# Hybrid HGRN2/mLSTM layer with a seven-product SwiGLU network: product order in a block, finer steps at the network's seams, scan steps moved

## Chip, cores and metric

One core of one Trainium2 chip runs one denoising step of one layer. The metric is the device time of an execution in microseconds, the median of several runs. The shapes are fixed: 128 context tokens and 1024 latent tokens (1152 in all, nine tiles of 128), model width 1024, network width 2816 (22 blocks of 128), everything in fp32.

## The reference, cut to what matters

Each token is normalised and modulated, projected into two groups of heads (four HGRN2 heads, four mLSTM heads, both scanned forward and backward in chunks), the heads' outputs are normed and gated and projected back, and a SwiGLU network follows. Context and latent tokens take different modulation rows; the latent scans start from cached states.

```python
def trunk_layer(x, cond, ...):
    mod = (jax.nn.silu(cond) @ w_mod_l + b_mod_l)[:, None, :]
    sh1, sc1, g1, sh2, sc2, g2 = jnp.split(mod, 6, axis=-1)
    h = rmsnorm(x, n1) * (1.0 + sc1) + sh1
    mix, new_states = token_mix(h, ...)      # projection, two scans, head norms, w_out
    x = x + g1 * mix
    h = rmsnorm(x, n2) * (1.0 + sc2) + sh2
    ffn = (jax.nn.silu(h @ w_gate_l) * (h @ w_up_l)) @ w_down_l
    x = x + g2 * ffn
    return x, new_states
...
y_prompt = rmsnorm(xp, final_norm_w)
y_sample = rmsnorm(xs, final_norm_w)
```

## The kernel before

Every large matmul is made of three fp32r matmuls: each operand is cast by ScalarE to a high part, VectorE subtracts that from the original for a low part, and TensorE adds up high*high, high*low and low*high in one PSUM bank (`three`, `product`). PSUM is cut into three banks for the pool `psA` and five for `psB`.

The program has five stages. In the first (`ORDER0`) the tokens are normed, transposed and modulated and the first projection runs. In the second (`ORDER`) the other projections, the convolution, both scans and the late modulation rows (`late_mod`) are steps with names such as `m.0.E.0`: head kind, head, step, third of the tokens. Both orders are strings of step names written out by hand; the steps are emitted in that order, and a scheduler then places the instructions of each engine in its own queue by dependencies and priorities that follow the order of emission. `m.h.E.r` only issues two loads on SyncE's queue (`eb` and `qt`, rows of `rows_d` spread over partitions), which `m.h.O1.r` needs on VectorE; `out.i.q` loads half of a tile of mixed heads and splits it. The third stage is the output projection (`out_main`, `po` in PSUM) with the residual, the second norm, the transposes (`nt` in PSUM) and the modulation of each tile in `out_post`.

The fourth and fifth stages are the network, in two passes of 22 blocks: p=0 with 640 tokens, p=1 with 512. A block works on its 2x2 split in a scheme with seven products instead of eight (`block`, matmuls at L1285, `gu` in PSUM). The left operands are the tokens (a11, a12, a22 and the sums s1 to s4, built by `left_build`), the right ones the weights (b11, b21, b22 and the sums t1 to t4, built by `right_build`). The left tiles have names beginning with `a_` and `s_`, and the right ones are `Tb` for a pair whose first member is a plain block of weights and `Tt` for a pair that begins with a sum. Pairs of right operands share a buffer of two tags (`wh`, `wl`), and the sums t1 to t4 are written to DRAM (`t_d`) in pass 0 and loaded from there in pass 1 by GpSimd's queue. `r` are the raw weights in a ring of four buffers, `wraw`.

A block's code calls, after each product, one of the seven pieces of the next block's `right_build` (`nx`), one down-projection `unit` of the group before (six matmuls, `dn` in PSUM, added to `acc` by VectorE) and the `extra` pieces of that place, `more(0)` to `more(6)`. The last product's evacuation (`finish`) and two pieces of `right_build` are run at the head of the next block. The tiles 7 and 8 are finished inside block 0 of pass 0: `out_post(7)` at `more(2)`, `out_post(8)` at `more(6)`. All seven pieces of `left_build(1)`, for pass 1, stand among the ten last down units of pass 0. At the end, `last` takes each of eight final down units from PSUM: a multiply by the gate row `g2` into `y`, an add to `acc`, a square on ScalarE, and for each tile the reciprocal root on GpSimd, two multiplies by it and `fnrow` (L128), and the store. `residual` multiplies what has been added up by `g2` and adds the residual row `x1`; half of these steps stand between the last down units.

## Time and profile before

| what | value |
|---|---|
| median of 3 runs | 1663.03 us (1661.39 to 1663.47) |
| the profiled execution | 1657.22 us, of which the span of the trace is 1655.4 us |
| TensorE busy | 1586.9 us (96% of the span) |
| VectorE busy | 1196.2 us (72%) |
| ScalarE busy | 696.3 us (42%) |
| stages, us from the start | first 0 to 55, scans to 750, output projection to 852, pass 0 to 1281, pass 1 and tail to 1655.4 |

The profile is of one execution. A sum of parts is made against its own time, 1657.22 us, and carried to the median by the difference. The page shows the whole span in slices; the timeline gives the instructions of a stretch in order of time, with what ended the idle time before each; the windows view gives busy time and TensorE's granted clock of any stretch. Matmuls are pipelined, so a row of twelve matmuls with 1.92 us is followed by the next 1.76 us after its start.

### The profile page before, as it was taken

The page shows a single profiled execution, that of the slowest core. Times are in us where ns is not written, and L with a number is a line of the kernel's source. Part 1 is how long each engine was busy: PE and PEld are TensorE (multiplying, and loading weights), DVE is VectorE, ACT ScalarE, POOL GpSimd, SP SyncE. Part 2 cuts the span into 40 slices and gives each one's busy share as a digit, 9 for nine tenths or more (in the row PEclk, how much of TensorE's full clock was granted, in tenths as well). Part 3 has the DMA queues.
Part 4 walks back from the last instruction along what each step waited for, and adds up shares of the span by engine and source line. Part 5 has one row for each costly group of instructions (what it writes and reads, how often), then busy time and mean ns, then how long its engine had stood idle before and what let it go on. Part 6 is the DMA issues. An engine that isn't in the chain of part 4 may idle for free.

```text
span 1655.4 us, 31292 instructions
## 1 busy us (share of the span) xinstructions
PE 1586.9 (96%) x11993; PEld 1434.6 (87%) x11993; DVE 1196.2 (72%) x2620; ACT 696.3 (42%) x1657; POOL 152.0 (9%) x264
## 2 busy tenths in 40 slices
PE   7999999999999989989989999999999999999996
PEld 5998898988898989857768999999998999999995
DVE  6765676577985776765666888888887866766677
ACT  6623433354454545453655433333434343333332
POOL 1000000000010000001111111111111111111110
PEclk9999999999999999999999999999999999999998
DMA  8312213112243234365457665556567677877762
GB/s 325 115 31 73 78 56 92 54 56 88 89 137 101 65 76 93 83 196 175 134 190 244 212 204 187 192 184 202 180 202 242 217 230 244 257 229 240 240 209 96
DMA packets 123466, 261.51 MB, mean 158 GB/s; under 512 B 12444, under 2 KB 39476, under 8 KB 122292
## 3 DMA queue, kind: packets, MB, share of 16 engines
q1 hardware_dynamic: 90916, 155.69, 30.2%
q0 software_dynamic: 28176, 101.73, 18.6%
q10 hardware_dynamic: 4224, 2.10, 0.4%
q8 instruction: 94, 1.54, 0.4%
q14 instruction: 56, 0.46, 0.1%
HBM read 194.69 MB, written 64.77 MB: 157 GB/s over the span
## 4 chain that ended last, share of the span: by engine, by line
PE 80%; DVE 7%; DMA 6%; issue 3%; ACT 2%; POOL 1%; SPq 0%; another core or an unknown queue 0%; DVEq 0%; POOLq 0%; ACTq 0%
PE gu L1285 28%; PE dn L135 16%; PE pv L135 5%; PE po L984 5%; PE zm L135 5%; PE zg L135 3%; PE zb L135 2%; DMA qt<-rows_d 2%; PE zo L135 2%; DMA wm<-in_dram 2%; PE zq L135 2%; PE zf L135 2%; PE z L333 2%; PE lm L196 1%; PE mo L891 1%
## 5 line engine op out<-in xcount | busy, mean ns | idle before, releaser
L135 PE MATMUL dn<-hid 128*128 128x512 f32 x1188 | 306.9, 395 | 4.4 <-ACT hid L1292 4.2
L135 PEld LDWEIGHTS dn<-hid 128*128 128x128 f32 x1188 | 214.2, 189 | 41.3 <-ACT hid L1292 5.4
L1285 PE MATMUL gu<-s,Tb 128*128 128x320 f32 (+1 forms) x1584 | 235.1, 297 | 0.8 <-ACT Tb L1096 0.6
L1285 PEld LDWEIGHTS gu<-s,Tb 128*128 128x128 f32 x1584 | 222.5, 190 | 6.4 <-ACT Tb L1096 0.9
L125 DVE TENSOR_TENSOR tmp<-gu,tmp 128x320 f32<-128x320 f32 (+1 forms) x308 | 136.2, 454 | 72.0 <-PE gu L1285 69.5
L1096 ACT CAST Tb<-r 128x512 fp32r<-128x512 f32 x176 | 106.9, 620 | 144.7 <-PE gu L1285 79.4
L1285 PE MATMUL gu<-a,Tb 128*128 128x320 f32 (+1 forms) x1056 | 156.4, 297 | 0.0
L1285 PEld LDWEIGHTS gu<-a,Tb 128*128 128x128 f32 x1056 | 148.8, 190 | 3.8
L125 DVE TENSOR_TENSOR acc<-acc,dn 128x512 f32<-128x512 f32 x172 | 117.8, 685 | 22.2 <-PE dn L135 22.1
L119 DVE TENSOR_TENSOR Tb<-r,Tb 128x512 fp32r<-128x512 f32 x176 | 119.6, 688 | 17.8 <-ACT Tb L1096 15.0
L984 PE MATMUL po<-wo_A,mix 128*128 128x512 f32 x288 | 95.6, 405 | 2.0 <-ACT mix L213 1.5
L1255 ACT CAST hid<-raw_dn 128x512 fp32r<-128x512 f32 x88 | 52.7, 618 | 73.0 <-PE dn L135 62.4
L135 PE MATMUL pv<-wh_v,h_hi 128*128 128x256 f32 (+1 forms) x288 | 82.8, 288 | 0.0
L135 PE MATMUL pv<-wl_v,h_hi 128*128 128x256 f32 (+1 forms) x288 | 82.2, 286 | 0.0
L135 PE MATMUL pv<-wh_v,h_lo 128*128 128x256 f32 (+1 forms) x288 | 81.8, 284 | 0.0
L128 DVE SCALAR_TENSOR_TENSOR qk<-pad,sm,qk 128x384 f32<-128x384 f32 (+1 forms) x144 | 78.3, 570 | 0.9
L1285 PEld LDWEIGHTS gu<-a,Tt 128*128 128x128 f32 x528 | 74.8, 189 | 3.3
L1285 PEld LDWEIGHTS gu<-s,Tt 128*128 128x128 f32 x528 | 74.8, 189 | 3.3
L1285 PE MATMUL gu<-a,Tt 128*128 128x320 f32 (+1 forms) x528 | 77.3, 296 | 0.0
L1285 PE MATMUL gu<-s,Tt 128*128 128x320 f32 (+1 forms) x528 | 77.3, 296 | 0.0
L168 POOL TENSOR_TENSOR rs_f<-ms_f,half 128x3 f32<-128x3 f32 x24 | 22.8, 949 | 532.7 <-DVE ms_f L166 495.1
L119 DVE TENSOR_TENSOR hid<-raw_dn,hid 128x512 fp32r<-128x512 f32 x88 | 60.3, 688 | 11.7 <-ACT hid L1255 11.7
(338 smaller groups left out, 3456.3 us busy)
## 6 DMA issues: line engine op xcount, KB each, us to landing
r<-in_dram SPq DMA_DIRECT2D x154, 256.0 KB, 4.1
t_d<-Tb POOLq DMA_DIRECT2D x44, 512.0 KB, 3.8
raw_dn<-in_dram SPq DMA_DIRECT2D x88, 256.0 KB, 3.1
t_d<-Tt POOLq DMA_DIRECT2D x44, 512.0 KB, 4.6
Tb<-t_d POOLq DMA_DIRECT2D x44, 512.0 KB, 4.7
Tt<-t_d POOLq DMA_DIRECT2D x44, 512.0 KB, 5.9
wm<-in_dram SPq DMA_DIRECT2D x64, 256.0 KB, 3.8
wm<-in_dram SPq DMA_DIRECT2D x8, 1024.0 KB, 7.9
```

Of the source, the lines that this page charges most:

```text
L119: V.tensor_tensor(out=out, in0=a, in1=b, op=ALU.subtract)
L125: V.tensor_tensor(out=out, in0=a, in1=b, op=ALU.add)
L128: V.scalar_tensor_tensor(out=out, in0=a, scalar=s, in1=b, op0=op0, op1=op1)
L135: E.matmul(ps, a, b, start=(i == 0), stop=(i == n - 1))
L168: G.tensor_tensor(out=rs, in0=ms, in1=half[:, 0:n], op=ALU.pow)
L196: E.matmul(ps[32 * j:32 * j + 32, :], cT[:, 4 * g + j, :], rhs, start=(g == 0), stop=(g == 1), tile_position=(0, 32 * j))
L333: E.matmul(first[b][r], x, y, start=(k == 0 and n == 0), stop=(k == KD - 1 and n == 2))
L891: E.matmul(po[:, d, :], eb[:, d, cs], v[:, c, :], start=True, stop=(ch == 0))
L984: E.matmul(ps[n], mt[:, a, k, :], b[:, k, nn], start=(k == 0 and m == 0), stop=(k == KD - 1 and m == 2))
L1096: S.copy(hi, src)
L1255: S.copy(hi, draw[u, n])
L1285: E.matmul(ps, rt[:, x, k, :], lt[:, y, k, :], start=(n == 0), stop=(n == 11))
```

## The change

1. The seven products of a block stand in another order. Before: a11 b11, s2 t2, a12 b21, s3 t3, s1 t1, a22 t4, s4 b22. After: a11 b11, a12 b21, s2 t2, s3 t3, s1 t1, a22 t4, s4 b22. The pairs of right operands become (b11, b21), (t2, t3), (t1, t4), (b22); the split of b21 moves from the third piece of `right_build` to the second, t2 from the second to the third. `left_build` is cut into ten pieces, with a11 and a12 first.
2. `out_post` is cut in two; the transposes and the modulation become `out_turn`. In block 0 `out_post(7)` stands at place 1, `out_turn(7)` at 4, `out_post(8)` at 5, and `out_turn(8)` at place 1 of block 1.
3. Seven pieces of `left_build(1)` stay among the last down units of pass 0, now behind the unit's add; three move to places 0 to 2 of block 0 of pass 1.
4. At the end, the last two blocks of `w_dn` are multiplied by the `g2` row before their split (four VectorE multiplies), and `last` is one add from PSUM. The other half of the residual steps moves into the last block (two of four in its places, two behind it). The last units run tile by tile, 8, 8, 7, 7, 6, 6, 5, 5.
5. Both tables of steps are permuted by a few places; `m.0.E.0`, for instance, stood behind `m.0.KV.0` and now stands behind `m.1.zm.1.2`.

The number of matmuls is the same, and so is that of transfers of `t_d`; VectorE has four instructions fewer at the end.

```diff
-lateb.10 late.11.B m.1.cv.1.0 m.0.KV.0 m.0.E.0 vproj.2.4 m.0.E.1 m.1.cv.1.1 m.0.O1.0 m.0.O1.1 vproj.2.8
+vload.2 g.3.zg.1 m.1.zm.1.0 g.3.O.1 g.3.zg.2 lateb.9 m.1.zm.1.1 m.1.zm.1.2 m.0.E.0 late.10.B g.3.F.0 m.0.states
...
-    slots = {"a11": "a12", "s2": "s3", "a12": "s1", "s3": "a22", "a22": "s4", "s4": "s2", "s1": "a11"}
+    slots = {"a11": "s2", "a12": "s3", "s2": "s1", "s3": "a22", "a22": "s4", "s4": "a12", "s1": "a11"}
...
-        def first():
+        def sums():
             for a, ks in ext_parts(p):
                 add(a, source(p, 1, 0)[:, ks, :], source(p, 1, 1)[:, ks, :])
-            left_split(p, "a11", one(0, 0))
-
-        def second():
+
+        def differences():
             sub(source(p, 1, 0), source(p, 0, 0), source(p, 1, 0))
             for a, ks in ext_parts(p):
                 sub(source(p, 0, 0)[:, ks, :], a, source(p, 0, 0)[:, ks, :])
-            left_split(p, "s2", one(0, 0))
-
-        def third():
-            left_split(p, "a12", one(0, 1))
-            sub(source(p, 0, 1), source(p, 0, 1), source(p, 0, 0))
-
-        return [first, second, third, lambda: left_split(p, "s3", one(1, 0)), lambda: left_split(p, "a22", one(1, 1)),
+
+        return [lambda: left_split(p, "a11", one(0, 0)), lambda: left_split(p, "a12", one(0, 1)), sums, differences,
+                lambda: left_split(p, "s2", one(0, 0)),
+                lambda: sub(source(p, 0, 1), source(p, 0, 1), source(p, 0, 0)),
+                lambda: left_split(p, "s3", one(1, 0)), lambda: left_split(p, "a22", one(1, 1)),
                 lambda: left_split(p, "s4", one(0, 1)), lambda: left_split(p, "s1", ext_parts(p))]
...
         def first():
-            right_pair(u, "wh", ("b11", "t2"))
+            right_pair(u, "wh", ("b11", "b21"))
...
         def second():
+            right_split(u, "b21", r("r21"))
             if not again:
                 sub(r("r11"), r("r22"), r("t1"))
+                sub(r("r12"), r("r22"), r("r12"))
+
+        def third():
+            right_pair(u, "wl", ("t2", "t3"))
             summed("t2", wraw.get((u, "r11")))
-
-        def third():
-            right_pair(u, "wl", ("b21", "t3"))
-            right_split(u, "b21", r("r21"))
-            if not again:
-                sub(r("r12"), r("r22"), r("r12"))
-
-        def fourth():
             if not again:
                 sub(r("r21"), r("r21"), r("r11"))
+
+        def fourth():
             summed("t3", wraw.get((u, "r12")))
...
     def down_split(u, f, n):
         hi, lo = down_of(f, n)
+        if u >= 2 * NF - 2:
+            mul(draw[u, n], draw[u, n], g2[1][:, n * 512:n * 512 + 512])
         S.copy(hi, draw[u, n])
...
     def last(i, n, ps):
         nn = slice(n * 512, (n + 1) * 512)
-        y = fp.tile([P, 512], F32, tag="rw", name="y%d_%d" % (i, n), bufs=4)
-        mul(y, ps, g2[1][:, nn])
-        add(acc_of(i, nn), acc_of(i, nn), y)
+        add(acc_of(i, nn), acc_of(i, nn), ps)
...
             if p == 0 and f == 0:
-                extra.setdefault(2, []).append(lambda: out_post(NT - 2))
-                extra.setdefault(6, []).append(lambda: out_post(NT - 1))
+                extra.setdefault(1, []).append(lambda: out_post(NT - 2))
+                extra.setdefault(4, []).append(lambda: out_turn(NT - 2))
+                extra.setdefault(5, []).append(lambda: out_post(NT - 1))
+            if p == 0 and f == 1:
+                extra.setdefault(1, []).append(lambda: out_turn(NT - 1))
...
-            if p == 1 and f == NF - 1:
+            if p == 1 and g == NG - 1:
                 for j, i in enumerate(tiles_of(p)):
-                    extra.setdefault(1 + j, []).append(lambda i=i: x1_load(i, 0))
-                    extra.setdefault(3 + j, []).append(lambda i=i: residual(i, 0))
+                    extra.setdefault(j, []).append(lambda i=i: x1_load(i, odd))
+                    if not odd or j < 2:
+                        extra.setdefault(j + 3, []).append(lambda i=i: residual(i, odd))
...
-            pend = None
-            for i, n in ((8, 0), (7, 0), (8, 1), (7, 1), (6, 0), (5, 0), (6, 1), (5, 1)):
-                if n:
-                    x1_load(i, 1)
-                ps = down_unit(p, g, i, n, True)
-                if n:
-                    residual(i, 1)
-                last(i, n, ps)
+            for i in tiles_of(p)[2:]:
+                residual(i, 1)
+            for i in tiles_of(p):
+                for n in range(2):
+                    last(i, n, down_unit(p, g, i, n, True))
```

TensorE's queue at the start of the network, before: `gu_0` are the products of block 0, told apart by their left operand, and the two `nt` are the halves of tile 7's transposes.

```order
L1285 MATMUL gu_0_9649<-a_0_9341,Tb_0_9452 128x320 x12
L1285 MATMUL gu_0_9663<-s_0_9347,Tb_0_9452 128x320 x12
L1285 MATMUL gu_0_9677<-a_0_9442,Tb_0_9561 128x320 x12
L1178 MATMUL nt_0_9708<-con,xj_9695 128x128
L1178 MATMUL nt_1_9718<-con,xj_9695 128x128
L1285 MATMUL gu_0_9730<-s_0_9446,Tb_0_9561 128x320 x2
L1178 MATMUL nt_0_9708<-con,xj_9695 128x128
```

The same place after:

```order
L1291 MATMUL gu_0_9649<-a_0_9337,Tb_0_9452 128x320 x12
L1291 MATMUL gu_0_9663<-a_0_9340,Tb_0_9452 128x320 x12
L1291 MATMUL gu_0_9691<-s_0_9442,Tt_0_9561 128x320 x12
L1291 MATMUL gu_0_9710<-s_0_9446,Tt_0_9561 128x320 x12
L1291 MATMUL gu_0_9728<-s_0_9556,Tt_0_9628 128x320 x12
L1180 MATMUL nt_0_9746<-con,xj_9676 128x128
L1180 MATMUL nt_1_9756<-con,xj_9676 128x128
L1291 MATMUL gu_0_9768<-a_0_9449,Tt_0_9628 128x320 x5
```

Two products stood whole behind the first one ahead of the transposes of tile 7, and now four do.

TensorE's queue at the head of block 1, after; `dn_0` are down units of group 0, which need `hid` of block 0, and the `nt` here are tile 8's transposes (before, these stood at once behind block 0's last product):

```order
L1291 MATMUL gu_0_9803<-s_0_9553,Tb_0_9635 128x320 x11
L1291 MATMUL gu_1_9819<-a_0_9337,Tb_1_9704 128x320 x12
L1291 MATMUL gu_1_9851<-a_0_9340,Tb_1_9704 128x320 x12
L135 MATMUL dn_0_4_0_10034<-hid 128x512 x2
L135 MATMUL dn_0_3_0_10067<-hid 128x512 x2
L135 MATMUL dn_0_2_0_10093<-hid 128x512
L1180 MATMUL nt_0_9868<-con,xj_9788 128x128
L1180 MATMUL nt_1_9878<-con,xj_9788 128x128
```

Two whole products and five matmuls of down units now stand between block 0's last product and tile 8's transposes.

VectorE's queue in block 12 of pass 0, before: `Tb_13_12028` is the low part of b21 of block 13 (from `r_13_11930`, the raw r21).

```order
L125 TENSOR_TENSOR tmp_0_9647<-gu_12_11933,tmp_0_9647 128x320
L119 TENSOR_TENSOR Tb_13_11972<-r_13_11869,Tb_13_11972 128x512
L125 TENSOR_TENSOR acc<-acc,dn_5_4_0_11946 128x512
L119 TENSOR_TENSOR r_13_11869<-r_13_11928,t_13_11975 128x512
L119 TENSOR_TENSOR hid<-raw_dn_1_11956,hid 128x512
L125 TENSOR_TENSOR tmp_0_9648<-gu_12_11959,tmp_0_9647 128x320
L119 TENSOR_TENSOR Tb_13_11972<-r_13_11869,Tb_13_11972 128x512
L125 TENSOR_TENSOR acc<-acc,dn_5_3_0_11977 128x512
L125 TENSOR_TENSOR tmp_0_9647<-gu_12_11987,tmp_0_9647 128x320
L119 TENSOR_TENSOR Tb_13_12028<-r_13_11930,Tb_13_12028 128x512
```

After, where b21 is the second half of `Tb_13_11973`:

```order
L125 TENSOR_TENSOR tmp_0_9648<-gu_12_11933,tmp_0_9647 128x320
L119 TENSOR_TENSOR Tb_13_11973<-r_13_11869,Tb_13_11973 128x512
L125 TENSOR_TENSOR acc<-acc,dn_5_4_0_11946 128x512
L119 TENSOR_TENSOR Tb_13_11973<-r_13_11930,Tb_13_11973 128x512
L119 TENSOR_TENSOR r_13_11869<-r_13_11928,t_13_11976 128x512
L125 TENSOR_TENSOR tmp_0_9647<-gu_12_11960,tmp_0_9647 128x320
```

The subtraction that needs r21 stood behind the evacuations of the second and third products of block 12 (`gu_12_11959`, `gu_12_11987`), and now it stands ahead of that of the third one emitted (`gu_12_11960`), with one down unit's add between the evacuation before it and itself.

VectorE's queue at the end, before, from the first of the last down units:

```order
L122 TENSOR_TENSOR y_0_17638<-dn_10_8_0_17631,g2row 128x512
L122 TENSOR_TENSOR y_0_17651<-dn_10_7_0_17644,g2row 128x512
L125 TENSOR_TENSOR acc<-acc,y_0_17638 128x512
L125 TENSOR_TENSOR acc<-acc,y_0_17651 128x512
L122 TENSOR_TENSOR y_1_17668<-dn_10_8_1_17659,g2row 128x512
L125 TENSOR_TENSOR acc<-acc,x_8_1_17657 128x512
L122 TENSOR_TENSOR y_1_17693<-dn_10_7_1_17684,g2row 128x512
L125 TENSOR_TENSOR acc<-acc,y_1_17668 128x512
L122 TENSOR_TENSOR y_0_17713<-dn_10_6_0_17706,g2row 128x512
L125 TENSOR_TENSOR acc<-acc,x_7_1_17682 128x512
L125 TENSOR_TENSOR fsq_17641<-fsq_17641 128x1
L125 TENSOR_TENSOR acc<-acc,y_0_17713 128x512
```

After:

```order
L125 TENSOR_TENSOR acc<-acc,dn_10_8_0_17651 128x512
L119 TENSOR_TENSOR hid<-tmp_1_13913,hid 128x256
L125 TENSOR_TENSOR acc<-acc,dn_10_8_1_17662 128x512
L125 TENSOR_TENSOR acc<-acc,dn_10_7_0_17681 128x512
L125 TENSOR_TENSOR fsq_17659<-fsq_17659 128x1
L166 TENSOR_SCALAR ms_fin_17673<-fsq_17659 128x1
L128 SCALAR_TENSOR_TENSOR acc<-acc,rs_fin_17675,fnrow 128x512 x2
L125 TENSOR_TENSOR acc<-acc,dn_10_7_1_17692 128x512
L125 TENSOR_TENSOR acc<-acc,dn_10_6_0_17710 128x512
L125 TENSOR_TENSOR fsq_17689<-fsq_17689 128x1
L166 TENSOR_SCALAR ms_fin_17703<-fsq_17689 128x1
L125 TENSOR_TENSOR acc<-acc,dn_10_6_1_17721 128x512
```

The multiplies into `y` and the adds of `x` are gone from this stretch.

## Rows read from the trace of the kernel before

**Rows 1.** The page's first two parts: busy time of each engine with its share of the span and its instructions, and TensorE's granted clock in 40 slices of the span, in tenths of full speed.

```profile
PE 1586.9 (96%) x11993; PEld 1434.6 (87%) x11993; DVE 1196.2 (72%) x2620; ACT 696.3 (42%) x1657; POOL 152.0 (9%) x264
...
PEclk9999999999999999999999999999999999999998
```

**Rows 2.** The windows view by stage: length of the stretch, then busy us (and instructions) of TensorE, its weight loads, VectorE, ScalarE and GpSimd, the granted clock, the DMA share and GB/s.

```profile
55.00:750.00 695.00, 665.98 (x6311) 605.76 (x6310) 488.51 (x1283) 301.79 (x872) 35.49 (x46) 0.99 0.31 87
750.00:852.00 102.00, 100.57 (x452) 76.66 (x451) 58.82 (x83) 51.92 (x111) 11.54 (x20) 1.00 0.51 165
852.00:900.00 48.00, 37.79 (x233) 34.49 (x232) 31.51 (x59) 25.64 (x53) 6.54 (x12) 0.93 0.63 213
900.00:1277.00 377.00, 377.00 (x2236) 351.50 (x2235) 307.42 (x559) 147.20 (x281) 42.68 (x80) 1.00 0.61 202
1277.00:1284.00 7.00, 4.29 (x18) 3.19 (x17) 7.00 (x12) 4.42 (x8) 0.00 (x0) 0.90 0.60 210
1284.00:1639.00 355.00, 355.00 (x2424) 329.89 (x2422) 255.37 (x506) 124.81 (x257) 48.59 (x90) 1.00 0.69 221
1639.00:1655.40 16.40, 0.07 (x1) 0.00 (x0) 10.51 (x21) 2.52 (x8) 2.02 (x3) 0.56 0.42 160
```

**Rows 3.** The same view of short stretches in which, or just behind which, TensorE waited.

```profile
690.00:695.00 5.00, 5.00 (x19) 3.07 (x16) 0.96 (x1) 1.41 (x5) 0.00 (x0) 0.50 0.33 118
860.00:865.00 5.00, 0.00 (x0) 0.00 (x0) 3.69 (x6) 3.76 (x6) 1.63 (x3) 0.78 0.34 138
865.00:870.00 5.00, 3.90 (x16) 2.94 (x17) 1.86 (x4) 3.33 (x9) 1.14 (x2) 0.54 0.48 185
1280.00:1283.00 3.00, 1.83 (x7) 1.53 (x8) 3.00 (x7) 2.39 (x4) 0.00 (x0) 0.94 0.23 81
1283.00:1286.00 3.00, 3.00 (x10) 2.44 (x9) 3.00 (x6) 0.46 (x1) 0.00 (x0) 0.50 0.57 191
```

**Rows 4.** The timeline of the start of the feed-forward network: start in us, duration in us, engine, line, operation, output and inputs, shape, count, and in brackets the engine's idle time before it and what ended that.

```profile
852.93 1.92 PE L1285 MATMUL gu<-a,Tb 128*128 128x320 f32 x12
...
855.22 0.86 SPq L1163 DMA_DIRECT2D xj<-in_dram  x2
...
859.95 1.23 DVE L125 TENSOR_TENSOR xj<-xj 128x1024 f32<-128x1024 f32 x1 [0.58 <-DMA xj<-in_dram]
...
861.21 1.06 ACT L1170 ACTIVATE xj<-xj 128x1024 f32<-128x1024 f32 x1 [3.95 <-DVE xj L125]
...
862.10 1.22 DVE L125 TENSOR_TENSOR xj<-xj 128x1024 f32<-128x1024 f32 x1
...
864.16 0.57 POOL L168 TENSOR_TENSOR rs_n<-ms_n,half 128x1 f32<-128x1 f32 x1
...
865.30 0.75 DVE L1172 TENSOR_SCALAR xj<-xj,rs_n 128x1024 f32<-128x1024 f32 x1
...
866.10 0.69 PE L1178 MATMUL nt<-con,xj 128*128 128x128 f32 x2 [7.74 <-DVE ms_n L166]
```

**Rows 5.** The timeline at the end of the network's first block and in its second.

```profile
887.68 1.92 PE L1285 MATMUL gu<-s,Tb 128*128 128x320 f32 x12
...
889.44 1.92 PE L1285 MATMUL gu<-a,Tb 128*128 128x320 f32 x12
...
896.63 0.73 PE L135 MATMUL dn<-hid 128*128 128x512 f32 x2 [1.50 <-ACT hid L1292]
```

**Rows 6.** The timeline of the seam between the network's two passes.

```profile
1272.00 1.22 DVE L125 TENSOR_TENSOR ext<-src 128x1024 f32<-128x1024 f32 x1 [2.56 <-DMA src<-hB_d]
...
1280.14 0.49 DVE L122 TENSOR_TENSOR tmp<-tmp,tmp 128x320 f32<-128x320 f32 x1
...
1281.17 3.83 PE L135 MATMUL dn<-hid 128*128 128x512 f32 x11 [2.71 <-ACT hid L1292]
```

**Rows 7.** The timeline of the end of the program.

```profile
1627.84 11.23 PE L135 MATMUL dn<-hid 128*128 128x512 f32 x48
...
1630.25 1.38 DVE L122 TENSOR_TENSOR y<-dn,g2row 128x512 f32<-128x512 f32 x2 [0.26 <-PE dn L135]
...
1645.33 0.69 DVE L125 TENSOR_TENSOR acc<-acc,x 128x512 f32<-128x512 f32 x1
...
1646.84 0.63 ACT L1403 ACTIVATE fjk<-acc 128x512 bf16<-128x512 f32 x1 [0.60 <-DVE fsq L125]
...
1649.55 0.55 POOL L168 TENSOR_TENSOR rs_fin<-ms_fin,half 128x1 f32<-128x1 f32 x1 [1.85 <-DVE ms_fin L166]
1650.13 1.41 DVE L128 SCALAR_TENSOR_TENSOR acc<-acc,rs_fin,fnrow 128x512 f32<-128x512 f32 x2 [0.73 <-POOL rs_fin L168]
```

**Rows 8.** The timeline at three places of the scan phase.

```profile
533.92 0.96 DVE L122 TENSOR_TENSOR qt<-qt,qk 128x768 f32<-128x768 f32 x1 [0.73 <-DMA qt<-rows_d]
...
617.58 0.80 PE L891 MATMUL mo<-v,eb 128*128 128x130 f32 x2 [3.93 <-DVE eb L128]
...
689.59 1.07 PE L196 MATMUL lm<-wm,cT 128*32 128x256 f32 x4 [3.54 <-DMA wm<-in_dram]
```

**Rows 9.** The timeline of an undisturbed block of pass 0 (the SPq row is four DMA issues, the last of them at its end), and behind it the page's sixth part for the same loads: issues, KB each, median us from issue to landing.

```profile
1077.97 9.63 SPq L1087 DMA_DIRECT2D r<-in_dram  x4
...
1090.28 0.69 DVE L125 TENSOR_TENSOR acc<-acc,dn 128x512 f32<-128x512 f32 x1
...
r<-in_dram SPq DMA_DIRECT2D x154, 256.0 KB, 4.1
```

103 lines of the change are left out of this document (57 added, 46 removed).

## The prediction, made before the changed kernel ran

> **What bounds the kernel now.** I read the page's shares first. TensorE is busy 1586.9 us of the 1655.4 us span, so all its waits together are 68.5 us; VectorE has 72% and ScalarE 42% [rows 1]. The share says nothing of where the waits are, so the windows view by stage comes next. In the network's two passes TensorE is busy 377.00 of 377 us and 355.00 of 355 us [rows 2]: no instruction that is taken from another engine there can save time, and the new product order has as many matmuls as the old. What can be saved lies in four places: 10.2 us idle in the 48 us at the start of the network (37.79 busy), 2.7 us between the passes (4.29 of 7), 16.3 us behind the last matmul, and 29.0 us scattered over the 695 us of projections and scans [rows 2]. Then I read what a wait costs beyond itself. Behind each longer one the granted clock shows half speed, 1.2 instead of 2.4 GHz, for some us: 0.54 in 865 to 870, 0.50 in 1283 to 1286, 0.50 in 690 to 695 [rows 3]. With 3.90 us busy at 0.54 the first of these lost some 3.90 x 0.46 = 1.8 us of work at full speed, the second 1.5 us, the third 2.5 us.
>
> **Start of the network.** Before, the first product starts at 852.93, products follow each other 1.76 us apart (887.68, 889.44), and three of them stand ahead of the transposes of tile 7; TensorE has done these at 858.4 and stands until 866.10, 7.74 us [rows 4, 5]. The chain that ends there is the load of the residual (issued 855.22), the add at 859.95, the square at 861.21, GpSimd's root at 864.16, the multiply at 865.30 [rows 4]. After, five products stand ahead, since a12 b21 and s3 t3, s1 t1 do not need tile 7: the fifth is done at 852.93 + 5 x 1.76 + 0.16 = 861.9. The chain still begins with the same load, so it is not much earlier. It loses one piece: tile 8's add (862.10, 1.22 us), which stood on VectorE between tile 7's square and its mean, is now emitted later. From the square's end (862.3) I count 0.5 us for the read of the sum and the mean, 0.57 us root, 0.75 us multiply and some 0.4 us of handing over, which gives transposes at 864.5, a wait of 2.6 us; if the chain gains nothing, 866.1 and 4.2 us. I take 3: minus 4.7 us. The clock I leave as it is, since a wait of 2.71 us at 1281.17 was followed by half speed as well [rows 3, 6]; 0 to minus 1.8. The Trainium skill, in TensorE: Matmul & The Clock Gate, section HAM oscillation, warns only of idle gaps in front of TensorE that are long enough, and by that rule the shortened wait could leave the clock up and the sum would be 1.8 us lower; the row at 1281 speaks against it.
>
> Behind it a second wait of 1.50 us stood at 896.63, where the first down units wanted `hid` of block 0, 7.2 us after that block's last product had ended at 889.4 [rows 5]. Now five matmuls of such units stand only two products (3.5 us) behind it, ahead of tile 8's transposes, and whatever they wait for holds up these too. Against that, tile 8's residual and norm are now worked off before block 0's last product ends, instead of on VectorE and ScalarE just where `hid` is made. Bounds: 0 us, or 7.2 - 3.5 = 3.7 us; I take the 1.5 us that it has now. Of the 10.2 us of this stretch about 4.5 stay: **minus 5.7 us**, from minus 9 to minus 2.
>
> **Seam between the passes.** VectorE is busy for all of the 7 us [rows 2]; it starts on the sums when the last part of the sources lands at 1272.00 and reaches the multiply for `hid` at 1280.14, and TensorE waits 2.71 us for that [rows 6]. In the new order of VectorE the same four operations of 1.22 us lie between these two (a sum, two differences, the low part of a12), one split of weights less and one of down weights more, both of 128x512. So **0 us**, from minus 4.2 (wait and clock gone, 2.7 + 1.5) to plus 1.5. The three pieces that move into block 0 of pass 1 stand beside full TensorE work in a pass in which VectorE is idle for 28% (255.37 of 355 us) [rows 2]; without that cover each would cost its 1.22 us.
>
> **The end.** TensorE's last 48 matmuls run from 1627.84 to 1639.07, 1.40 us for a unit of six. VectorE works on to 1651.54, and the span ends 3.9 us behind it [rows 7]. VectorE is what is late: for each unit a multiply and an add of 0.69 us, for half of them a residual add, and for each tile 1.41 us of L128. The change takes eight multiplies and four residual adds out of this stretch: 12 x 0.69 = 8.3 us, if VectorE stays the limit. It doesn't, since the units now end 1.40 us apart and an add takes 0.69, so I built the end forward: the last add is done at 1639.8, tile 6's L128 at 1641.3 to 1641.8 (tile 5's square of 0.63 us lies beside it), two small operations and the root of 0.55 us bring 1642.7 to 1643.2, L128 1644.1 to 1644.6, the store 1648.0 to 1648.5: minus 7.2 us. What is taken out is added elsewhere: four multiplies of `w_dn` and four residual adds, 8 x 0.69 = 5.5 us of VectorE, in the last two blocks, where it has some 4.5 us free in each ((355 - 255.37) / 22) [rows 2]. The last two residual adds stand ahead of `hid` in its queue and can put the last units off by 0 to 1.4 us; I take 1. **Minus 6 us**, from minus 4 to minus 7.5.
>
> **Blocks.** TensorE is full, so **0 us** [rows 2]. The split of b21 is moved forward past a product's evacuation. It needs r21, whose load is the last of four issues that end at 1087.60 and lands 4.1 us later in the median, at 1091.7; after the cast VectorE could go on at 1092.3, but comes to it behind the first unit's add, at 1091.0 [rows 9]. It would stand some 1.3 us in each block of 19.3 us (7 x 1.76 + 5 x 1.40), in which it has 18.5% idle (307.42 of 377 us), 3.6 us [rows 2]. That idle time and the spare banks of `psB` are the cover; the rival below says what it costs without.
>
> **Scan steps.** The two largest waits are 3.93 us at 617.58 (a scan product that waits for VectorE) and 3.54 us at 689.59 (the load of late modulation weights) [rows 8]. The second has the same order on TensorE's and SyncE's queues after, so it stays with its clock. Near the first only a few steps trade places. Where steps move most, at 530, `m.0.E.0` issues its two loads some steps earlier, and VectorE's wait for `qt` (0.73 us at 533.92) goes with the small waits of TensorE around it. I take **minus 2 us**; the bounds are plus 3 (one more wait like the one at 689.59) and minus 6 (the first large one gone, with its clock).
>
> **Sum.** -5.7 + 0 - 6 + 0 - 2 = -13.7 us: the profiled 1657.22 would become 1643.5. That execution is 5.8 us below the median, so from 1663.03 I forecast 1649.3, given as 1649, with its own range from 1644 to 1655.
>
> **Rivals.** (1) More: the seam between the passes closes too and the first large scan wait goes; 1649 - 4.2 - 4 = 1641. For it speaks that the operations for a11 and a12 come first; against it the count on VectorE's queue. (2) Less: down units moved forward wait 3.7 us, the end gains only 4 and the permuted steps bring new waits of 3 us; 1649 + 2.2 + 2 + 5 = 1658. For it speaks that the order was changed in places with no wait too. (3) The change does nothing where it aims: tile 7's chain is as late as before and is found again behind the fifth product, and the freed VectorE time at the end is lost to a later start of the last units; some 1663 with the loss of the scans. (4) Slower: VectorE stands in each block of pass 0 for r21. It decides from a wait of 3.6 us, if loads land 2.3 us later than their median; past that every microsecond costs the 20 blocks 20 us, so with 1 us too much 1649 + 20 = 1669.
>
> **Chances.** Forecast 0.58, (1) 0.15, (2) 0.14, (3) 0.07, (4) 0.06. The range from 1641 to 1659 leaves out (3), (4) and the lower half of (1). A measurement of this kernel can tell 0.2%, some 3.3 us, from no change: faster is below 1659.7, slower above 1666.4. Faster 0.86, the same 0.08, slower 0.06.
>
> **What would show it.** In the profile after: a wait of 2 to 4 us ahead of tile 7's transposes behind five products, where 7.74 stood; no wait over 2 us ahead of the first down units; TensorE busy in all of both passes; some 9 us instead of 16.3 between the last matmul and the span's end; the wait between the passes unchanged near 2.7. Wrong would be: a TensorE wait that repeats in every block, VectorE waiting over 3.6 us for r21's cast, or scan waits whose sum is not near 27 us.

## The result, and the profile after

| | before | after |
|---|---|---|
| median | 1663.25 us (1661.39 to 1666.22, 4 runs) | 1644.14 us (1641.65 to 1645.97, 4 runs) |
| profiled execution, its span | 1657.22, 1655.4 us | 1643.06, 1641.3 us |

The ratio is 0.9882, interval 0.9862 to 0.9903: the changed kernel is faster by 1.2%, by 19.1 us between the medians and by 14.2 us between the two profiled executions. Forecast were 13.7 us and a median of 1649.

The two traces, cut at the same landmarks:

| stretch | before | after | difference | forecast |
|---|---|---|---|---|
| start of the program to the network's first product | 852.93 | 849.06 | -3.87 | -2 |
| from there to the wait between the passes | 425.54 | 420.91 | -4.63 | -5.7 |
| the wait between the passes | 2.71 | 1.81 | -0.90 | 0 |
| from its end to the end of the last matmul | 357.89 | 359.96 | +2.07 | 0 |
| from there to the end of the span | 16.33 | 9.56 | -6.77 | -6 |
| sum | 1655.40 | 1641.30 | -14.10 | -13.7 |

The page's shares and TensorE's clock in 40 slices, after; they answer to [rows 1]:

```profile
PE 1585.9 (97%) x11993; PEld 1433.9 (87%) x11993; DVE 1189.7 (72%) x2616; ACT 692.1 (42%) x1657; POOL 152.0 (9%) x264
...
PEclk9999999999999999999999999999999999999999
```

TensorE works as long as before (1585.9 against 1586.9 us), so 13.1 of the 14.1 us are waits: 55.4 us of them are left of 68.5. The windows view by stage says where, columns as in [rows 2]:

```profile
55.00:750.00 695.00, 668.86 (x6324) 607.12 (x6323) 490.17 (x1284) 303.68 (x876) 36.36 (x47) 0.99 0.31 87
...
852.00:900.00 48.00, 42.14 (x259) 38.85 (x258) 32.96 (x63) 26.70 (x56) 6.95 (x12) 0.96 0.71 239
900.00:1269.00 369.00, 369.00 (x2190) 344.19 (x2190) 303.57 (x552) 143.27 (x276) 42.66 (x80) 1.00 0.61 203
...
1284.00:1632.00 348.00, 346.24 (x2387) 322.44 (x2385) 247.77 (x501) 120.52 (x257) 48.76 (x91) 1.00 0.71 227
1632.00:1641.30 9.30, 0.00 (x0) 0.00 (x0) 4.47 (x11) 1.45 (x4) 1.10 (x2) 0.59 0.41 169
```

The 48 us at the start of the network lost 5.9 us of idle time where they had lost 10.2; pass 0 is full as before; pass 1, full before, has 1.8 us of waits; the tail is down to 9.56 us. The timeline of the start of the network, after (it answers to [rows 4, 5]):

```profile
849.06 3.69 PE L1291 MATMUL gu<-a,Tb 128*128 128x320 f32 x24
...
852.58 5.44 PE L1291 MATMUL gu<-s,Tt 128*128 128x320 f32 x36
...
859.10 0.44 PE L1180 MATMUL nt<-con,xj 128*128 128x128 f32 x2 [1.08 <-DVE xj L1168]
...
861.28 1.73 SPq L1084 DMA_DIRECT2D r<-in_dram  x2
...
864.65 3.68 PE L1291 MATMUL gu<-a,Tb 128*128 128x320 f32 x24
864.85 0.49 DVE L125 TENSOR_TENSOR tmp<-gu,tmp 128x320 f32<-128x320 f32 x1
...
870.03 0.69 DVE L119 TENSOR_TENSOR t<-r,r 128x512 f32<-128x512 f32 x1 [4.69 <-DMA r<-in_dram]
...
871.16 0.46 ACT L1298 CAST hid<-tmp 128x320 fp32r<-128x320 f32 x1 [4.85 <-DVE tmp L122]
...
872.55 2.07 PE L135 MATMUL dn<-hid 128*128 128x512 f32 x4 [4.21 <-ACT hid L1298]
```

Five products (24 and 36 matmuls of twelve each) stand ahead of tile 7's transposes, which wait 1.08 us instead of 7.74. But at 872.55 the down units that were moved forward wait 4.21 us, and the reading goes back in one chain: TensorE for ScalarE's cast of `hid`, ScalarE for VectorE's multiply, and VectorE, from 865.34 to 870.03, for the raw weights of block 2, of which `t` (the sum t1) is the difference. Their loads were issued from 861.28 to 863.01, and VectorE can go on 7.0 us after that, where [rows 9] have 4.1 from issue to landing in the median. The windows view of that stretch shows VectorE and GpSimd idle and the DMA engines full:

```profile
861.00:866.00 5.00, 5.00 (x35) 4.50 (x34) 4.27 (x8) 4.10 (x11) 2.17 (x4) 1.00 0.75 209
866.00:870.00 4.00, 2.33 (x16) 2.07 (x15) 0.00 (x0) 0.30 (x1) 0.00 (x0) 1.00 1.05 366
870.00:875.00 5.00, 2.45 (x6) 1.86 (x7) 4.88 (x11) 3.22 (x7) 1.24 (x2) 0.76 0.83 293
```

The clock column (third from the end) is 1.00 behind the 1.08 us wait and 0.76 behind the 4.21. The wait between the passes, and pass 1 where loads of `t_d` are late:

```profile
1271.79 3.68 PE L135 MATMUL dn<-hid 128*128 128x512 f32 x8 [1.81 <-ACT hid L1298]
...
1300.33 1.66 PE L1291 MATMUL gu<-s,Tt 128*128 128x256 f32 x12 [0.99 <-DMA Tt<-t_d]
...
1305.70 1.55 PE L1291 MATMUL gu<-a,Tt 128*128 128x256 f32 x11 [0.33 <-DMA Tt<-t_d]
```

And the end, which answers to [rows 7]:

```profile
1620.64 11.10 PE L135 MATMUL dn<-hid 128*128 128x512 f32 x48
...
1623.17 0.69 DVE L125 TENSOR_TENSOR acc<-acc,dn 128x512 f32<-128x512 f32 x1 [0.43 <-PE dn L135]
...
1633.55 1.42 DVE L128 SCALAR_TENSOR_TENSOR acc<-acc,rs_fin,fnrow 128x512 f32<-128x512 f32 x2
...
1635.37 0.55 POOL L168 TENSOR_TENSOR rs_fin<-ms_fin,half 128x1 f32<-128x1 f32 x1 [1.85 <-DVE ms_fin L166]
1635.95 1.41 DVE L128 SCALAR_TENSOR_TENSOR acc<-acc,rs_fin,fnrow 128x512 f32<-128x512 f32 x2 [0.73 <-POOL rs_fin L168]
```

VectorE now waits for TensorE at the first unit, and it ends 1637.36 - 1631.74 = 5.6 us behind the last matmul, where it had ended 12.5 us behind (1651.54 against 1639.07 [rows 7]). In the scans, the wait at 617.58 [rows 8] is 2.19 us instead of 3.93, and that for the modulation weights 3.66 instead of 3.54.

### The profile page after: what moved, and what is told of

It is laid out like the page before. It is cut to its first block, busy times and chain, and to the rows that moved or that the text cites. A ratio compares the mean times of both kernels' runs of the same rounds, so it can differ in the third digit from the quotient of the medians.

```text
span 1641.3 us, 31210 instructions
## 1 busy us (share of the span) xinstructions
PE 1585.9 (97%) x11993; PEld 1433.9 (87%) x11993; DVE 1189.7 (72%) x2616; ACT 692.1 (42%) x1657; POOL 152.0 (9%) x264
## 4 chain that ended last, share of the span: by engine, by line
PE 47%; DMA 3%; DVE 2%; issue 1%; ACT 0%; POOL 0%; SPq 0%; DVEq 0%; POOLq 0%; ACTq 0%
PE gu L1291 28%; PE dn L135 16%; PE po L984 3%; DMA r<-in_dram 1%; DMA Tt<-t_d 1%; DMA src<-hB_d 1%; PE nt L1180 1%; DMA hB_d<-xj 0%; DMA g1row<-g_d 0%; DVE acc L128 0%; DMA xj<-in_dram 0%; DVE tmp L125 0%; DMA mix_d<-on 0%; DVE acc L125 0%; DMA raw_mx<-mix_d 0%
## 5 line engine op out<-in xcount | busy, mean ns | idle before, releaser
L1291 PEld LDWEIGHTS gu<-s,Tt 128*128 128x128 f32 x1584 | 224.6, 190 | 11.5 <-DVE tmp L125 1.2
L1291 PE MATMUL gu<-s,Tt 128*128 128x320 f32 (+1 forms) x1584 | 232.3, 296 | 1.2 <-DMA Tt<-t_d 1.2
L1291 PE MATMUL gu<-a,Tb 128*128 128x320 f32 (+1 forms) x1056 | 147.9, 296 | 0.0
L1291 PEld LDWEIGHTS gu<-a,Tb 128*128 128x128 f32 x1056 | 143.4, 190 | 0.2
L1093 ACT CAST Tb<-r 128x512 fp32r<-128x512 f32 x132 | 81.0, 616 | 56.6 <-PE gu L1291 26.3
L119 DVE TENSOR_TENSOR Tb<-r,Tb 128x512 fp32r<-128x512 f32 x132 | 90.5, 686 | 12.7 <-ACT Tb L1093 10.7
L1108 POOL DMA_DIRECT2D t_d<-Tt x88 | 47.0, 535 | 345.5 <-DVE Tt L119 327.4
L1291 PE MATMUL gu<-s,Tb 128*128 128x320 f32 (+1 forms) x528 | 77.8, 296 | 0.0
L1291 PEld LDWEIGHTS gu<-s,Tb 128*128 128x128 f32 x528 | 73.7, 190 | 1.7
L1105 POOL DMA_DIRECT2D Tt<-t_d x88 | 47.1, 539 | 258.6 <-PE gu L1291 257.2
```

The costliest lines, as they stand in the source:

```text
L119: V.tensor_tensor(out=out, in0=a, in1=b, op=ALU.subtract)
L1093: S.copy(hi, src)
L1105: G.dma_start(right[u, nm], dst)
L1108: G.dma_start(dst, right[u, nm])
L1291: E.matmul(ps, rt[:, x, k, :], lt[:, y, k, :], start=(n == 0), stop=(n == 11))
```

## The experiments

All kernels compute everything. "Stretch" is the time from the network's first product to the wait between the passes, "tail" the time from the last matmul to the end of the span.

**The four parts taken back one at a time.** Each is the changed kernel with one part as before.

Old product order (`e1_old_products`):

```diff
-            right_pair(u, "wh", ("b11", "b21"))
+            right_pair(u, "wh", ("b11", "t2"))
...
-        product(p, u, "a12", "b21", ps)
+        product(p, u, "s2", "t2", ps)
```

> The changed kernel with the product order of before (s2 t2 second, a12 b21 third, and the pieces of the right operands that go with it); all else as changed. My theory: the transposes of tile 7 moved behind five products because the residual's steps were cut and moved, not because of the product order, so the start of the network keeps its gain; in the emitted order no down units stand ahead of tile 8's transposes any more, so the 4.2 us wait for hid of block 0 shrinks, and the waits for t_d loads at the start of pass 1 (1.5 us) go, while the wait between the passes grows by 1: 2 to 5 us faster than the changed kernel, span 1636 to 1640. Rival, that the product order carries the gain at the network's start: tile 7's transposes wait 5 us or more again, span 1644 to 1647.

Measured: 1641.97 us, ratio 0.9887 (0.9867 to 0.9907), span 1640.2, just past the theory's end; by the ratio it is no faster than the changed kernel, where I had expected 2 to 5 us. The transposes of tile 7 wait 1.57 us and stand behind five products here too. Undone, the order costs nothing, so the sum that gave it a part of the start of the network is refuted: the place in the code (`more(4)`) sets the five, and no left operand that is multiplied there needs tile 7 in the old order either.

Steps of tiles 7 and 8 uncut, at their old places (`e2_old_seam`):

```diff
-                extra.setdefault(1, []).append(lambda: out_post(NT - 2))
-                extra.setdefault(4, []).append(lambda: out_turn(NT - 2))
-                extra.setdefault(5, []).append(lambda: out_post(NT - 1))
-            if p == 0 and f == 1:
-                extra.setdefault(1, []).append(lambda: out_turn(NT - 1))
+                extra.setdefault(2, []).append(lambda: (out_post(NT - 2), out_turn(NT - 2)))
+                extra.setdefault(6, []).append(lambda: (out_post(NT - 1), out_turn(NT - 1)))
```

> The changed kernel with the residual, norm and transposes of tiles 7 and 8 as one piece each at the places of before (2 and 6 of block 0); all else as changed. My theory: TensorE waits 6 to 8 us ahead of tile 7's transposes behind three products, and the 4.2 us wait for hid falls to 1 to 2: span 1644 to 1648 against 1641.3. Rival, that the product order carries the gain: span within 1 us of 1641.3.

Measured: 1645.70 us, ratio 0.9905 (0.9883 to 0.9926). In the timeline of this kernel both old waits are back:

```profile
857.46 0.69 PE L1180 MATMUL nt<-con,xj 128*128 128x128 f32 x2 [5.06 <-DVE xj L1168]
...
889.01 0.73 PE L135 MATMUL dn<-hid 128*128 128x512 f32 x2 [2.59 <-ACT hid L1298]
```

The stretch is 425.44 us, as before the change (425.54). The cut is all that the start of the network gained. The profiled span, 1640.9, hides it: this execution came to its first product at 846.95, 2.1 us earlier than the changed kernel's, and had no wait for `Tt` in pass 1.

Old end (`e3_old_end`):

```diff
-        if u >= 2 * NF - 2:
-            mul(draw[u, n], draw[u, n], g2[1][:, n * 512:n * 512 + 512])
...
-        add(acc_of(i, nn), acc_of(i, nn), ps)
+        y = fp.tile([P, 512], F32, tag="rw", name="y%d_%d" % (i, n), bufs=4)
+        mul(y, ps, g2[1][:, nn])
+        add(acc_of(i, nn), acc_of(i, nn), y)
```

(The residual steps and the order of the last units are also those of before.)

> The changed kernel with the end of before (multiply by g2 behind each last down unit, half of the residual steps among them, units in the old order); all else as changed. My theory: VectorE's surplus behind the last matmul comes back whole, 16 us instead of 9.6 between the last matmul and the end, the last matmul 0 to 1 us earlier: span 1647 to 1648.5. Rival, that half of the gain comes from elsewhere (a better start of the last units): span 1644 to 1645.

Measured: 1649.98 us, ratio 0.9929 (0.9910 to 0.9948), tail 16.32. The end is worth its 6.8 us and is not paid for earlier.

Old tables (`e4_old_tables`; `ORDER0` and `ORDER` of the kernel before, as far as shown in the change's diff):

```diff
-vload.2 g.3.zg.1 m.1.zm.1.0 g.3.O.1 g.3.zg.2 lateb.9 m.1.zm.1.1 m.1.zm.1.2 m.0.E.0 late.10.B g.3.F.0 m.0.states
+lateb.10 late.11.B m.1.cv.1.0 m.0.KV.0 m.0.E.0 vproj.2.4 m.0.E.1 m.1.cv.1.1 m.0.O1.0 m.0.O1.1 vproj.2.8
```

> The changed kernel with both step tables of before; all else as changed. My theory: the 3.9 us by which the network starts earlier (849.06 against 852.93) are the tables' alone: span 1645 to 1646, first product at 852.5 to 853.3. Rival, that they are scatter between executions: first product at 848 to 851, span 1640 to 1643.5.

Measured: 1648.05 us, ratio 0.9913 (0.9894 to 0.9932), first product at 855.22, later than the 852.5 to 853.3 that I had expected. The tables are worth 4 to 6 us, more than the 2 that I gave them.

**Inside two parts.** Without the multiply of the down weights, with eight multiplies at the end instead (`e5_gate_late`):

```diff
-        if u >= 2 * NF - 2:
-            mul(draw[u, n], draw[u, n], g2[1][:, n * 512:n * 512 + 512])
...
-        add(acc_of(i, nn), acc_of(i, nn), ps)
+        y = fp.tile([P, 512], F32, tag="rw", name="y%d_%d" % (i, n), bufs=4)
+        mul(y, ps, g2[1][:, nn])
+        add(acc_of(i, nn), acc_of(i, nn), y)
```

> The changed kernel with the multiply by g2 back behind each last down unit (eight of 0.69 us from PSUM) instead of ahead of the split of the last weights (four); the residual steps and the order of units stay as changed. Theory, that VectorE's work behind the units sets the end: eight units of 1.38 us and four tiles of 1.71 us are 17.9 us from the first unit's end on, so the tail behind the last matmul grows from 9.6 to 12 to 14 us, span 1643.5 to 1645.5. Rival, that the order tile by tile does it: tail 9.5 to 10.5, span within 1 us of 1641.3.

Measured: 1649.05 us, ratio 0.9935 (0.9911 to 0.9959), tail 13.39. Of the 6.8 us the multiplies give 3.8 and the moved residual steps and the order of the units 3.0.

The sum t1 of block 2 on GpSimd, so that VectorE does not stand at it (`e6_t1_pool`):

```diff
-                sub(r("t1"), r("r12"), r("r11"))
+                (G if u in (2,) else V).tensor_tensor(out=r("t1"), in0=r("r12"), in1=r("r11"), op=ALU.subtract)
```

> The changed kernel with one operation moved: the difference t1 of block 2 (of the two raw weights that VectorE waits 4.69 us for, ahead of hid of block 0) runs on GpSimd instead. Theory, that hid is late because VectorE's queue stands on that load: the 4.2 us wait of the first down units falls under 1 us, and the span by 3 to 5.5 us with the clock (0.76 in 870 to 875), to 1636 to 1638. Rival, that the wait moves to the next operation that needs the late load, or that hid is late by itself: some other wait of 2 us or more appears in blocks 0 to 1, span 1640 to 1642.

Measured: 1641.70 us, ratio 0.9885 (0.9860 to 0.9910), stretch 419.87. TensorE's timeline and then VectorE's in this kernel:

```profile
871.93 1.32 PE L135 MATMUL dn<-hid 128*128 128x512 f32 x5
...
883.72 2.04 PE L1291 MATMUL gu<-s,Tb 128*128 128x320 f32 x12 [1.70 <-DVE tmp L125]
```

```profile
881.97 0.69 DVE L119 TENSOR_TENSOR r<-r,t 128x512 f32<-128x512 f32 x1 [6.64 <-DMA r<-in_dram]
```

The first down units start without a wait, here and in `e8_both` below, where the changed kernel and the five others with its code at this place wait 1.92 to 4.21 us: the cause is shown. The time is the rival's all the same (span 1641.1), and the stretch is only 1.0 us shorter, which is inside its scatter (418.4 to 422.8 us in all kernels with the cut). The clock fell here behind the transposes' wait of 1.41 us (0.66 in 862 to 867, against 1.00 in 861 to 866 in the changed kernel), and TensorE waits 1.70 us behind the 6.64 us for which VectorE stands at the next operation on the same block's raw weights. That stand is not new. The changed kernel's VectorE has it too, 4.72 us for another load, issued only from 875.79 us on:

```profile
880.85 0.69 DVE L119 TENSOR_TENSOR r<-r,t 128x512 f32<-128x512 f32 x1 [4.72 <-DMA r<-in_dram]
```

**Further tries.** More buffers for the late modulation weights, against the wait of 3.66 us at 689 (`e7_more_buffers`), and this together with t1 on GpSimd (`e8_both`):

```diff
-                raw = p15.tile([P, 2, 256], F32, tag="wmr", bufs=2, name="wm%d_%d_%d" % (part, g, jj))
+                tag, bufs = ("K", 3) if part >= 12 and g == 1 else ("wmr", 2)
+                raw = p15.tile([P, 2, 256], F32, tag=tag, bufs=bufs, name="wm%d_%d_%d" % (part, g, jj))
```

> The changed kernel in which the second half of each of the last four modulation loads (wm) gets buffers of a tag that is free by then, so that it needn't wait for the first half's matmuls. Theory, that the 3.66 us wait at 685 is the load's latency behind a buffer that comes free late, in both kernels: it goes with the half clock behind it (2.5 us), network starts 4 to 6 us earlier, span 1635 to 1637.5. Rival, that the SyncE queue or the DMA rate sets it: the wait moves to the weights of the output projection behind it and the network starts within 2 us of 849.

> The changed kernel with the difference t1 of block 2 on GpSimd and the additional buffers for the modulation loads. If both theories hold the two gains add up, 7 to 11 us below the changed kernel: span 1630 to 1634, median 1633 to 1637. If only one of them holds, 1636 to 1638.

Measured: 1643.93 us, ratio 0.9901 (0.9879 to 0.9924), and 1642.82, 0.9893 (0.9870 to 0.9916). In the first, the wait for `wm` at 689 is gone and the head norm stands in its place; in the second neither gain adds to the other. The first products come at 850.97 and 852.42 us, no earlier than the changed kernel's 849.06; behind the head norm stand a wait of 2.4 us for a later `wm` (722.76 in the first) and one of 2.3 us for another head norm (737.37), where the changed kernel has one of 2.49 us. In the first:

```profile
689.97 1.06 PE L405 MATMUL pt<-con,on 128*128 128x128 f32 x3 [3.04 <-ACT on L397]
```

**Each part alone on the kernel before.** The cut of the steps of tiles 7 and 8 alone (`e9_seam_only`; the diff is that of `e2_old_seam` read the other way, with `out_turn` as a function of its own):

```diff
-                extra.setdefault(2, []).append(lambda: out_post(NT - 2))
-                extra.setdefault(6, []).append(lambda: out_post(NT - 1))
+                extra.setdefault(1, []).append(lambda: out_post(NT - 2))
+                extra.setdefault(4, []).append(lambda: out_turn(NT - 2))
+                extra.setdefault(5, []).append(lambda: out_post(NT - 1))
+            if p == 0 and f == 1:
+                extra.setdefault(1, []).append(lambda: out_turn(NT - 1))
```

> The kernel before with only the cut of the residual steps of tiles 7 and 8 (steps into two pieces, four places); old products, old end, old tables. Theory (the cut alone is worth what the start of the network gave): from the first product of the network to the wait between the passes 425.5 before becomes 420.5 to 422.5; the wait for tile 7's transposes 7.7 becomes 1 to 4 us; a wait at block 0's down units may stay at 1 to 4 us; the tail stays at 16.3; by the profiles the span goes from 1655.4 to 1650 to 1652, ratio 0.996 to 0.998. Rival (the cut needs the new product order, with four products of cover instead of three): the stretch stays at 424 to 426 and the time within 1.5 us of before.

Measured: 1652.46 us, ratio 0.9960 (0.9945 to 0.9974), stretch 418.37. Its timeline:

```profile
861.77 1.92 PE L1293 MATMUL gu<-s,Tt 128*128 128x320 f32 x12
864.38 0.44 PE L1184 MATMUL nt<-con,xj 128*128 128x128 f32 x2 [0.69 <-DVE xj L1172]
...
876.51 0.63 PE L1293 MATMUL gu<-s,Tb 128*128 128x320 f32 x1 [2.02 <-ACT tmp L1335]
...
891.38 1.29 PE L135 MATMUL dn<-hid 128*128 128x512 f32 x3 [1.13 <-ACT hid L1300]
```

The fifth product (861.77) stands ahead of the transposes with the old order of products, too, and they wait 0.69 us: the cut alone does it. The stretch fell by 7.2 us, past what I expected (3 to 5).

The end alone (`e10_end_only`, the reverse of `e3_old_end`) and the product order alone (`e11_products_only`, with the new pieces of `left_build`):

```diff
-        y = fp.tile([P, 512], F32, tag="rw", name="y%d_%d" % (i, n), bufs=4)
-        mul(y, ps, g2[1][:, nn])
-        add(acc_of(i, nn), acc_of(i, nn), y)
+        add(acc_of(i, nn), acc_of(i, nn), ps)
```

> The kernel before with only the new end (multiply of the last two blocks' down weights ahead of their split, one add in place of multiply and add, residual steps moved, tile order). Theory: the tail from the last matmul to the span's end goes from 16.3 to 9.3 to 9.8 us, the last matmul ends within 2 us of before, so the span is 6 to 7 us shorter, ratio 0.9955 to 0.9970. Rival (the steps put into the last two blocks hold up the last units): the last matmul ends over 2 us later and the span is at most 4 us shorter.

> The kernel before with only the new order of products, the pairs of right operands, and the new pieces of the left operands; old tables, old end, residual steps uncut in their old places. Theory (worth nothing by itself): the stretch from the first product to the wait between the passes 424 to 427 against 425.5, span within 1.5 us of before apart from waits on loads, ratio 0.9985 to 1.0010. Rival (fewer products wait for tile 7, so the order gives the 4 to 6 us): the stretch 420 to 422, ratio 0.996 to 0.9975.

Measured: the end 1655.95 us, ratio 0.9963 (0.9947 to 0.9979), tail 9.53, last matmul at 1645.67; the product order 1658.26, ratio 0.9988 (0.9977 to 0.9999), stretch 426.30. The last matmul of the first ends 6.6 us later than in the trace of before, as the rival had it, but 5.35 us of this are there at the first product already (858.28, code that is as before) and 0.89 is a wait for a load of `Tt`; by the ratio the end gives 6.1 us, by the medians (1655.95 against 1660.77) 4.8.

Last, the changed kernel with three edits: those of `e7_more_buffers`, one head norm step behind a projection, and the last store in halves on two queues (`e12_best`):

```diff
-m.2.F.2 m.3.zo.1 out.0.0 m.3.zo.2
+m.3.zo.1 m.2.F.2 out.0.0 m.3.zo.2
...
-            if i == NT - 1:
-                Y.dma_start(y_sample[(i - 1) * P:i * P, qq], acc_of(i, qq))
+            if i in (NT - 1, 5):
+                (S if i == 5 and q else Y).dma_start(y_sample[(i - 1) * P:i * P, qq], acc_of(i, qq))
```

> The changed kernel with three more edits: the late modulation weights' second halves in buffers of their own (as in the run with more buffers), the head norm's step m.2.F.2 behind m.3.zo.1, and the last tile's store in two halves, each on its own queue as soon as its half is scaled. Theory: the head norm's wait of 3.0 us at 687 is gone with its half clock, first product of the network at 846 to 848.5 instead of 849.06, tail 8.3 to 9.2 instead of 9.56; span 1637 to 1640, ratio 0.985 to 0.9875. Rival (a wait moves on to the next late step, as it did twice): first product 849 to 851, tail 9.2 to 9.6, span 1640 to 1642, ratio 0.988 to 0.990.

Measured: 1643.83 us, ratio 0.9897 (0.9878 to 0.9917), tail 8.89, first product at 848.74. The split store gives its 0.7 us; at 686 the wait moved on once more:

```profile
689.89 2.97 PE L833 MATMUL mtk<-v,mkt 128*128 128x130 f32 x12 [3.60 <-ACT mkt L827]
```

The profiled execution (span 1637.7) was the fastest of five, and the median is no better than that of the changed kernel: no version here beats it by more than can be measured.

## Why the prediction was right, and where it was off

**The parts add up.** Taken alone, the ratios are 0.9960 for the cut, 0.9963 for the end and 0.9988 for the product order. The tables, from taking them back, 0.9913 against 0.9882, are 0.0031. Together 0.0040 + 0.0037 + 0.0012 + 0.0031 = 0.0120, and the whole change measured 0.0118. The first three have an interval of 0.001 to 0.002 to either side, the tables, as a difference of two ratios, some 0.003; that the sum meets the whole to 0.0002 is luck.

**Start of the network** (-5.7 forecast, -4.6 between the two traces). In the four profiled kernels without the cut the stretch is 425.4 to 426.3 us, mean 425.7; in the ten with it 418.4 to 422.8, mean 420.2. That is -5.5, the size forecast. Its parts were not: tile 7's transposes wait 1.08 us instead of the 3 forecast, since the chain through the root and the multiply brought them 10.0 us behind the first product (859.10 - 849.06) instead of 11.6 (864.5 - 852.93), and the clock stays at 1.00 behind it, where I had left it as it was. By the rule of the Trainium skill that I weighed, in TensorE: Matmul & The Clock Gate, section HAM oscillation, a shortened wait can leave the clock up; at this place the trace agrees (1.00 in 861 to 866). The length of the wait alone does not decide it in these runs: at this same place, with the same code, the clock fell behind 1.41 us in `e6_t1_pool` (0.66 in 862 to 867) and stayed at 1.00 behind 1.61 us in `e5_gate_late`, and elsewhere it fell behind 1.81 us (0.69 in 1270 to 1275) and 4.21 us (0.76 in 870 to 875). What came back is the wait of the down units: I took 1.5 us, with 3.7 as the bound and a part of the second rival, and the trace has 4.21, beyond the bound. The bound counted the time to make `hid` and took it that nothing stood in VectorE's way, of which [rows 5] show nothing; what stands there is a load that lands 7.0 us after its issue. `e6_t1_pool` shows this cause. The trace of before had such a wait of VectorE for the same kind of load in its block 0, and it could have been counted:

```profile
886.05 0.69 DVE L119 TENSOR_TENSOR r<-r,r 128x512 f32<-128x512 f32 x1 [5.31 <-DMA r<-in_dram]
```

In the two kernels with the cut and the old order of products the first down units stand later, at 886 to 891 (`e1_old_products`, `e9_seam_only`), and wait 1.1 to 1.2 us, behind a wait of 2.0 to 2.3 us at a product of the network's second block that waits for ScalarE; so early a place of the down units, and the wait of 2 to 4 us there, come with cut and new order together.

**The reason given for the five products was wrong.** "Five products stand ahead, since a12 b21 and s3 t3, s1 t1 do not need tile 7": they stand ahead in the old order as well (`e1_old_products`, `e9_seam_only`). The new order of products itself is worth 0 to 2 us (ratios 0.9887 against 0.9882 taken back, 0.9988 alone, whose interval goes to 0.9977). The gain came as forecast all the same, because the step that does it, the cut, is part of the same change.

**Seam between the passes** (0 forecast). 1.81 us after; with the three late pieces 1.77 to 2.97 us (the largest in two parts, in `e1_old_products`), with before's pieces 2.71, 3.11 and 3.22 (before, `e10_end_only`, `e9_seam_only`). If there is a gain it is under a microsecond, inside the bounds forecast. The waits for `Tt` behind it (+1.5 of the +2.07) do not go with the change: `e2_old_seam`, `e5_gate_late`, `e7_more_buffers` and `e8_both`, which have its order there, have none, and `e10_end_only`, which has before's, has one of 0.89.

**The end** (-6 forecast). Tail 9.50 to 9.56 us in the kernels with all of it, but for the one with the split store, and 16.32 to 16.39 in those without: -6.8. Built forward I had 7.2, less 1 for late last units; the 48 matmuls run through in 11.10 us (11.23 in [rows 7]), so the 1 us was not due.

**Blocks** (0 forecast). Pass 0 is busy 369.00 of 369 us; the rival of a wait for r21 in each block is refuted.

**Scan steps** (-2 forecast, -3.9 between the traces) is the mis-sized term. With the old tables five profiled executions reach the first product at 852.93, 855.22, 854.73, 858.28 and 852.23, mean 854.7; with the new ones six reach it at 849.06, 849.22, 846.95, 848.14, 848.76 and 851.26, mean 848.9: -5.8. (The three with other buffers for the modulation weights, 850.97, 852.42 and 848.74, are left out.) I had counted only waits among the scans. Their sum came near the forecast, from 55 to 750 us 26.1 us instead of 29.0, 27 forecast, and the one at 689 stayed, but the gain is at another place than I gave, so the sum was met by luck. I had put it near 530, where "VectorE's wait for `qt` (0.73 us at 533.92) goes with the small waits of TensorE around it", and nothing at 617, where "only a few steps trade places". The windows view of the two places, of the kernel before and then of the changed one:

```profile
525.00:550.00 25.00, 22.18 (x158) 20.17 (x158) 18.84 (x77) 14.80 (x54) 3.06 (x4) 1.00 0.42 132
605.00:640.00 35.00, 30.38 (x237) 29.50 (x237) 17.81 (x49) 16.48 (x61) 2.91 (x4) 0.95 0.28 53
```

```profile
525.00:550.00 25.00, 22.70 (x164) 20.59 (x164) 18.81 (x71) 15.86 (x57) 2.94 (x4) 1.00 0.42 130
605.00:640.00 35.00, 31.64 (x253) 30.57 (x252) 22.52 (x59) 19.07 (x71) 3.22 (x4) 1.00 0.44 81
```

In 525 to 550 TensorE stands 2.2 to 2.9 us in the five profiles with the old tables and 2.1 to 3.1 in the six with the new ones: nothing is gained. In 605 to 640 it stands 4.6 to 5.4 us with the old ones and 2.7 to 3.4 with the new ones, 2.0 less in the mean; the wait for `eb` there is 3.64 to 3.96 us with the old ones and 1.18 to 2.45 in all nine profiles with the new ones. Which of the moved steps does it was not tried. I had not counted the first table either, which orders the first 55 us, though TensorE stands 8.8 us there before the change. About 2 us lie there, and the other 1.8 of the 5.8 are not placed. The windows view from 20 to 30 us, of the kernel before, then of the one with the end alone, whose order is the same there, then of the changed kernel:

```profile
20.00:30.00 10.00, 8.00 (x70) 5.77 (x66) 7.76 (x21) 6.38 (x14) 0.55 (x1) 1.00 1.01 423
```

```profile
20.00:30.00 10.00, 8.14 (x56) 6.54 (x49) 5.99 (x17) 5.78 (x12) 0.56 (x2) 0.73 1.01 422
```

```profile
20.00:30.00 10.00, 8.17 (x69) 6.04 (x65) 7.68 (x21) 6.36 (x14) 0.55 (x1) 1.00 1.02 422
```

With the same order the clock stayed at 1.00 in one execution and fell to 0.73 in another, in which TensorE did 56 matmuls in its 8.14 us instead of 70. With the old tables it fell in four of five profiles (0.72, 0.83, 0.73, 0.76), and the one in which it stayed is the profile of before. With the new ones it fell in one of nine (0.75). The projections that follow, `zb`, start at 64.26 us in the first and at 66.2 to 67.9 in the four others (mean of the five 66.5), and at 63.4 to 67.0, mean 64.5, in the six with the new tables. The start goes with the clock: 66.2 to 67.9 us in the five profiles in which it fell, 63.4 to 64.8 in the nine in which it held.

**The step that carried the sum to the median** failed: "That execution is 5.8 us below the median, so from 1663.03 I forecast 1649.3". The sum itself was met, 1643.5 forecast and 1643.06 measured for the profiled execution, in part by luck: the scan steps gave 1.9 us more than forecast, the end 0.8 and the seam 0.9, the start of the network 1.1 less, and pass 1 lost 2.1. But the 5.8 us are not a constant that stays; the changed kernel's profile lies 1.1 us below its median. Some 2.9 of them (67.1, the mean of the four, less 64.26) may be the half clock at 20 to 30 us. And the 1663.03 was a median of three runs: in the 11, 11 and 29 executions of the kernel before that ran beside the later experiments the medians are 1662.03, 1659.22 and 1660.77, which lie only 2.0 to 4.8 us above the profiled execution. By means over profiles the change is -5.8 - 5.5 - 6.8 = -18.1 us, near the 19.1 between the medians. What in the new first table keeps the clock up was not tried by itself. One fall in nine profiles against four in five suggests that it goes with the tables; it does not show it, since three of those four were taken on one chip, on which there is a single profile with the new tables, and the kernel before itself was profiled only once.
